# First modulation vectors of a Hyena-FFN block: five of eight row tiles on TensorE, three on VectorE

## The chip, the cores and the metric

The kernel runs on one core of one Trainium2 chip. The metric is the device time of one execution in microseconds; lower is better.

## The reference

The whole block is one adaLN-modulated Hyena mixer followed by a gated convolutional FFN, on x of 1024 positions by 1024 channels. What the change touches is the beginning:

```
mod = silu(c) @ mod_w + mod_b          # (1024,) @ (1024, 6*1024): six vectors of 1024
sh1, sc1, g1, sh2, sc2, g2 = split(mod, 6)
h_lat = rmsnorm(x, norm_g[0]) * (1 + sc1) + sh1
proj = short_conv(h_lat @ w_in + b_in, ...)

# filter network, on 33 position features, width 64
h = sin(freq * (pos @ f_w1 + f_b1))
h = sin(freq * (h @ f_w2 + f_b2))
h = sin(freq * (h @ f_w3 + f_b3))
h = h @ f_wout                          # then a decay, an FFT convolution, and so on
```

## The kernel before

All of it is one program. Each engine works through its own list of instructions in order, and a scheduler makes these lists from the order in which the code is written; where one engine needs another's result it waits for a semaphore.

The program begins with three things woven into each other. The first is the filter network (`filter_mlp`): three layers, each over two halves of 512 positions. A half of a layer is a matmul into a PSUM bank `mlp`, an activation on ScalarE that scales and biases it (`pre`), the reduction of the phase to one period, and the sine (`hs`). The reduction rounds `pre`/(2 pi) by adding a large number and subtracting it again (`n`, lines 259 and 260, both on VectorE), subtracts `n` times 2 pi in two steps (line 262) and clamps (line 263). After the third layer the result is split into a rounded and a rest part, `s_h` and `s_l`.

The second is the first two modulation vectors (`mods_start`): chunk 1 of `mod` (the scale, kept as the tile `mod1`) and then chunk 0 (the shift, `mod0`). The matrix of a chunk comes in as 16 tiles of 128 rows by 512 columns; `mw1_20` is chunk 1, row tile 2, column half 0. TensorE multiplies six of the eight row tiles by silu(c) into a PSUM row per column half (`ms`), VectorE the other two (`DV0`, `DV1`) into `msa` (lines 337 and 339). Then VectorE adds the PSUM row into partition 0 of `msa` (line 329, the fold), eight matmuls with a column of ones (`mv`, line 348) sum over the partitions and turn the row into columns, and `mod_fin` adds the bias (line 300); for chunk 1 it also multiplies by the norm's weight (line 302). A float32 matmul stands in the trace as two passes, so ten `ms` matmuls are a row of x20.

The third is the normalization of the first four tiles of x (`first_pre`, `first_norm`): ScalarE squares and sums (`junk`, line 369), VectorE and ScalarE form the root and scale x (`n10r`, lines 356 to 377), TensorE transposes (`n10p`, line 384), and ScalarE and VectorE apply both modulation vectors (`n10t`) and split the result into `hTh` and `hTl`. With these the main matmuls begin (`in8p`), and they go on to the end of the program.

SP issues the loads in the order of the table `ORDER`: chunk 1, four tiles of x, chunk 0 with one weight tile in between, and so on. The two lines that say which row tiles VectorE takes are

```
DV0 = (6, 7)
DV1 = (0, 1)
```

Of the kernel before, what the change touches and what calls it, by code (L numbers as in the profile page):

```python
# [10 lines left out]
F32 = mybir.dt.float32  # L11
F32R = mybir.dt.float32r
AF = mybir.ActivationFunctionType
ALU = mybir.AluOpType
# [4 lines left out]
D = 1024  # L19
# [3 lines left out]
KT = D // 128  # L23
EPS = 1e-6
MAGIC = 12582912.0
# [2 lines left out]
PI_LO = 3.1415925  # L28


ORDER = [("m", 1, 0, 8), ("x", 0, 4), ("m", 0, 0, 6), ("w", 1), ("m", 0, 6, 8), ("w", 2), ("x", 4, 8)]
DV0 = (6, 7)
DV1 = (0, 1)
XA = (1, 5, 7)
OFF = {
    "k": (0, 1, 2, 2, 3), "s": (0, 1, 2, 2, 3), "a": (0, 1, 2, 4), "b": (0, 1, 2, 3, 3, 4, 4, 5, 5, 6),
# [11 lines left out]
class Kern:  # L48
# [188 lines left out]
    def filter_mlp(self):  # L237
        nc, a, sp = self.nc, self.a, self.sp
        fv = self.fv
# [6 lines left out]
            nc.vector.tensor_copy(out=s[0:64, :, 64:128], in_=zv)  # L246
            nc.vector.tensor_copy(out=s[64:128, :, 0:64], in_=zv)

        fb = self.cp.tile([128, 3], F32, name="fb")
        nc.vector.tensor_scalar(out=fb, in0=fv[:, 0:3], scalar1=fv[:, 3:4], scalar2=None, op0=ALU.mult)  # L250
        cur = [self.pos[hf][0:66] for hf in range(2)]
        for ly, w in enumerate(self.fw):
            for hf in range(2):
                p = self.bank("ax", f"mlp{hf}{ly}")
                nc.tensor.matmul(out=p, lhsT=w, rhs=cur[hf], start=True, stop=True)
                pre = self.rp(f"pre{hf}{ly}")[:, 0:512]
                nc.scalar.activation(out=pre, in_=p, func=AF.Identity, scale=fv[:, 3:4], bias=fb[:, ly:ly + 1])
                n = self.ftile("o", f"n{hf}{ly}")
                nc.vector.tensor_scalar(out=n, in0=pre, scalar1=1.0 / (2 * math.pi), scalar2=MAGIC, op0=ALU.mult, op1=ALU.add)
                nc.vector.tensor_scalar(out=n, in0=n, scalar1=MAGIC, scalar2=None, op0=ALU.subtract)  # L260
                for c in (C1, C2):
                    nc.vector.scalar_tensor_tensor(out=pre, in0=n, scalar=-c, in1=pre, op0=ALU.mult, op1=ALU.add)
                nc.vector.tensor_scalar(out=pre, in0=pre, scalar1=PI_LO, scalar2=-PI_LO, op0=ALU.min, op1=ALU.max)
                h = self.ftile("t1", f"hs{hf}{ly}", bufs=2)
                nc.scalar.activation(out=h, in_=pre, func=AF.Sin)
                cur[hf] = h
# [10 lines left out]
    def mod_gen(self, ch, tags):  # L277
        nc, a = self.nc, self.a
        acc = self.rp(f"macc{ch}") if self.fp else self.op.tile([128, D], F32, tag="bc0", name=f"macc{ch}")
        for kt in range(KT):  # L280
# [6 lines left out]
            if kt == KT - 1:  # L287
                if ch in (3, 4):
                    p = self.bank("ax", f"mv{ch}")
                    for j in range(KT):  # L290
                        nc.tensor.matmul(out=p[:, j:j + 1], lhsT=acc[:, j * 128:j * 128 + 128], rhs=self.ones[:, 0:1], start=True, stop=True)
                    self.mod_fin(ch, p)
                else:
                    self.mod_row(ch, acc)
            yield 1

    def mod_fin(self, ch, p):
        nc = self.nc
        t = self.mshift[ch]
        nc.vector.tensor_tensor(out=t, in0=p[:, 0:KT], in1=self.modb[:, ch], op=ALU.add)  # L300
        if ch in (1, 4):
            nc.vector.scalar_tensor_tensor(out=t, in0=t, scalar=1.0, in1=self.ng[:, ch // 4], op0=ALU.add, op1=ALU.mult)

    def mod_row(self, ch, acc):
        nc = self.nc
# [15 lines left out]
    def mods_start(self, ch, dv):  # L321
# [2 lines left out]
        acc = [self.ftile("hl"[h], f"msa{ch}{h}") for h in range(2)]  # L324
        pe = [kt for kt in range(KT) if kt not in dv]

        def fold():
            for h in range(2):
                nc.vector.tensor_tensor(out=acc[h][0:1], in0=ps[h][0:1], in1=acc[h][0:1], op=ALU.add)

        for kt in range(KT):
            if kt == dv[-1] > pe[-1]:
                fold()
            for h in range(2):
                wv = self.msw[ch, kt, h]
                if kt == dv[0]:
                    nc.vector.tensor_scalar(out=acc[h], in0=wv, scalar1=self.scl[:, kt:kt + 1], scalar2=None, op0=ALU.mult)
                elif kt in dv:
                    nc.vector.scalar_tensor_tensor(out=acc[h], in0=wv, scalar=self.scl[:, kt:kt + 1], in1=acc[h], op0=ALU.mult, op1=ALU.add)
                else:  # L340
                    nc.tensor.matmul(out=ps[h][0:1], lhsT=self.scl[:, kt:kt + 1], rhs=wv, start=kt == pe[0], stop=kt == pe[-1])
        if pe[-1] > dv[-1]:
            fold()
        p = self.bank("ax", f"mv{ch}")
        for h in range(2):
            for j in range(4):
                js = slice(j * 128, j * 128 + 128)
                nc.tensor.matmul(out=p[:, h * 4 + j:h * 4 + j + 1], lhsT=acc[h][:, js], rhs=self.ones[:, 0:1], start=True, stop=True)
        self.mod_fin(ch, p)

    def rstd(self, ss, n, name):
        nc, cp = self.nc, self.cp
# [41 lines left out]
    def first_loads(self):  # L394
# [7 lines left out]
        for step in ORDER:  # L402
# [4 lines left out]
                    self.nc.sync.dma_start(out=self.xin[t], in_=a["x"][t * 128:t * 128 + 128])  # L407
            else:
                _, ch, k0, k1 = step
                for kt in range(k0, k1):  # L410
                    for h in range(2):
                        w = self.htile(n // 4, n % 4 // 2, "hl"[n % 2], f"mw{ch}_{kt}{h}", F32)
                        n += 1
                        c0 = ch * D + h * 512
                        nc.sync.dma_start(out=w, in_=a["mod_w"][kt * 128:kt * 128 + 128, c0:c0 + 512])
                        self.msw[ch, kt, h] = w
        self.wo = self.sp.tile([128, D], F32, tag="delta", name="wo")
        nc.sync.dma_start(out=self.wo[0:64], in_=a["hy_f_wout"][:, 0:D])
        nc.sync.dma_start(out=self.wo[64:128], in_=a["hy_f_wout"][:, D:2 * D])
# [1096 lines left out]
```

## Time and profile before

| | |
|---|---|
| median of 3 runs | 1305.76 us (1305.61 to 1305.9) |
| profiled execution, its own time | 1301.95 us |
| its span, first to last instruction | 1300.2 us |
| TensorE matmul busy | 1232.0 us, 95% of the span |
| VectorE busy | 1063.9 us, 82% |
| ScalarE busy | 744.0 us, 57% |

The profiled execution is one run of the program; its span leaves out 1.75 us of its time that lie around the first and last instruction. A timeline lists one engine's instructions by start time, with those of one kind merged; in brackets stand the engine's idle time before them and what ended it. The table of stretches gives, for each stretch of time, how long each engine was busy, the clock that TensorE was granted (1.00 is the upper of its two levels, 0.50 the lower) and the mean busy share of the DMA engines.

### The profile page before, as it was taken

The page shows a single profiled execution, that of the slowest core. Times are in us where ns is not written, and L with a number is a line of the kernel's source. Part 1 is how long each engine was busy: PE and PEld are TensorE (multiplying, and loading weights), DVE is VectorE, ACT ScalarE, POOL GpSimd, SP SyncE. Part 2 cuts the span into 40 slices and gives each one's busy share as a digit, 9 for nine tenths or more (in the row PEclk, how much of TensorE's full clock was granted, in tenths as well). Part 3 has the DMA queues.
Part 4 walks back from the last instruction along what each step waited for, and adds up shares of the span by engine and source line. Part 5 has one row for each costly group of instructions (what it writes and reads, how often), then busy time and mean ns, then how long its engine had stood idle before and what let it go on. Part 6 is the DMA issues. An engine that isn't in the chain of part 4 may idle for free. (4 is left out here: it accounts for less than half of the span.)

```text
span 1300.2 us, 16048 instructions
## 1 busy us (share of the span) xinstructions
PE 1232.0 (95%) x5368; PEld 971.7 (75%) x5368; DVE 1063.9 (82%) x1351; ACT 744.0 (57%) x1215; POOL 353.2 (27%) x292
## 2 busy tenths in 40 slices
PE   7999989999899999999989999999999999998976
PEld 2687767777677777878768878888888878886865
DVE  7899875578786998796989998788778798977996
ACT  4798866677676878553644444444544454425442
POOL 2000011012100210000086445455445301521461
PEclk9999999999999999999989999999999999999988
DMA  9555699989989997543124431222222388646542
GB/s 339 191 156 156 209 287 285 275 251 269 270 253 301 273 302 263 175 154 128 51 83 129 161 129 65 98 81 76 87 81 82 130 286 307 232 154 219 197 144 97
DMA packets 112400, 241.35 MB, mean 186 GB/s; under 512 B 12436, under 2 KB 25620, under 8 KB 112318
## 3 DMA queue, kind: packets, MB, share of 16 engines
q1 hardware_dynamic: 96790, 226.83, 53.4%
q0 software_dynamic: 14848, 13.39, 4.9%
q8 instruction: 42, 0.69, 0.2%
q14 instruction: 40, 0.33, 0.1%
q10 hardware_dynamic: 680, 0.12, 0.0%
HBM read 186.29 MB, written 54.00 MB: 185 GB/s over the span
## 5 line engine op out<-in xcount | busy, mean ns | idle before, releaser
L1010 DVE SCALAR_TENSOR_TENSOR facc<-fpad,v_ffn_conv_w,facc 128x1024 f32<-128x1024 f32 x176 | 225.2, 1285 | 22.8 <-ACT facc L1005 19.2
L62 ACT ACTIVATE dh<-dr 128x512 fp32r<-128x512 f32 x132 | 75.7, 623 | 64.0 <-PE dB L58 23.4
L63 DVE TENSOR_TENSOR dl<-dr,dh 128x512 fp32r<-128x512 f32 x132 | 102.8, 825 | 4.2 <-ACT dh L62 4.0
L507 POOL DMA_DIRECT2D k_b<-in_k_b_dram x64 | 34.0, 532 | 263.6 <-PE ks L59 177.3
L973 POOL TENSOR_TENSOR s<-wrua 128x512 f32<-128x512 f32 x21 | 29.3, 1396 | 188.2 <-DVE s12l L963 95.6
L57 PE MATMUL dA<-dh,dh 128*128 128x512 f32 x176 | 69.7, 396 | 8.7 <-DVE p5fpad L1311 7.7
L58 PE MATMUL dA<-dl,dh 128*128 128x512 f32 x176 | 69.2, 393 | 2.0 <-DVE dl L63 2.0
L963 POOL TENSOR_TENSOR s43l<-s,s43h 128x1024 fp32r<-128x1024 f32 x21 | 50.4, 2399 | 68.5 <-ACT s43h L962 68.5
L59 PE MATMUL dA<-dh,dl 128*128 128x512 f32 x176 | 68.9, 392 | 0.0
L58 PE MATMUL dB<-dl,dh 128*128 128x512 f32 x132 | 52.2, 395 | 5.1 <-DVE dl L63 5.1
L59 PE MATMUL dB<-dh,dl 128*128 128x512 f32 x132 | 51.9, 393 | 0.0
L57 PE MATMUL dB<-dh,dh 128*128 128x512 f32 x132 | 51.9, 393 | 0.0
L58 PE MATMUL op<-wlo,qh 128*128 128x512 f32 x128 | 50.3, 393 | 0.0
L57 PE MATMUL op<-who,qh 128*128 128x512 f32 x128 | 50.0, 393 | 0.0
L59 PE MATMUL op<-who,ql 128*128 128x512 f32 x128 | 49.9, 390 | 0.0
L1005 ACT ACTIVATE facc<-fpad,v_ffn_conv_b,v_ffn_conv_w 128x1024 f32<-128x1024 f32 x22 | 26.6, 1210 | 37.4 <-DVE fpad L1073 37.3
L57 PEld LDWEIGHTS dA<-dh,dh 128*128 128x128 f32 x176 | 33.5, 191 | 16.4 <-issue 8.1
L286 DVE SCALAR_TENSOR_TENSOR macc<-mw,scl,macc 128x1024 f32<-128x1024 f32 x28 | 38.1, 1361 | 9.4 <-DMA mw<-in_mod_w_dram 9.2
L507 POOL DMA_DIRECT2D k_bi<-in_k_bi_dram x32 | 17.1, 534 | 103.3 <-PE zd L59 47.6
L962 ACT ACTIVATE s12h<-s 128x1024 fp32r<-128x1024 f32 x21 | 22.3, 1061 | 39.6 <-PE s L58 35.3
L974 POOL TENSOR_TENSOR s<-s,wrug 128x512 f32<-128x512 f32 x21 | 42.8, 2039 | 1.5
L573 ACT ACTIVATE who<-wro,invn 128x512 fp32r<-128x512 f32 x32 | 21.8, 717 | 37.1 <-PE op L59 28.7
(585 smaller groups left out, 4050.4 us busy)
## 6 DMA issues: line engine op xcount, KB each, us to landing
dr<-du SPq DMA_DIRECT2D x66, 256.0 KB, 3.7
dr<-in_ffn_w_down_dram SPq DMA_DIRECT2D x66, 256.0 KB, 4.6
mw<-in_mod_w_dram SPq DMA_DIRECT2D x32, 512.0 KB, 4.6
wrin<-in_hy_w_in_dram SPq DMA_DIRECT2D x24, 512.0 KB, 6.4
wrug<-in_ffn_w_up_dram SPq DMA_DIRECT2D x22, 512.0 KB, 3.4
wrua<-in_ffn_w_up_dram SPq DMA_DIRECT2D x22, 512.0 KB, 4.7
du<-fs SPq DMA_DIRECT2D x22, 512.0 KB, 2.6
mw<-in_mod_w_dram SPq DMA_DIRECT2D x32, 256.0 KB, 6.5
```

The costliest lines, as they stand in the source:

```text
L57: mm(out=out, lhsT=lh, rhs=rh, start=start, stop=False, **kw)
L58: mm(out=out, lhsT=lh, rhs=rl, start=False, stop=False, **kw)
L59: mm(out=out, lhsT=ll, rhs=rh, start=False, stop=stop, **kw)
L62: self.nc.scalar.activation(out=hi, in_=src, func=AF.Copy)
L63: self.nc.vector.tensor_tensor(out=lo, in0=src, in1=hi.bitcast(F32), op=ALU.subtract)
L286: nc.vector.scalar_tensor_tensor(out=acc, in0=w, scalar=self.scl[:, kt:kt + 1], in1=acc, op0=ALU.mult, op1=ALU.add)
L507: self.nc.gpsimd.dma_start(out=b, in_=self.a[name][k2])
L963: eng.tensor_tensor(out=l, in0=src, in1=h.bitcast(F32), op=ALU.subtract)
L973: tt(out=s12[:, lo], in0=a[:, lo], in1=a[:, hi], op=ALU.add)
L974: tt(out=s12[:, hi], in0=s12[:, lo], in1=g[:, lo], op=ALU.subtract)
L1005: nc.scalar.activation(out=av, in_=pad[:, 1:17, 1:65], func=AF.Identity, scale=self.cw[:, b, 4:5], bias=self.cb[:, b:b + 1])
L1010: nc.vector.scalar_tensor_tensor(out=av, in0=pad[:, dy:dy + 16, dx:dx + 64], scalar=self.cw[:, b, i:i + 1], in1=av, op0=ALU.mult, op1=ALU.add)
```

## The change

Row tiles move from TensorE to VectorE: of each chunk VectorE takes three and TensorE five. In the filter network the subtraction of the large number goes from VectorE to ScalarE, as an activation with a bias tile (`fb[:, 3:4]`, filled by a memset). `mod_fin` works on a slice of columns, and `mods_start` folds, multiplies by ones and finishes the first column half ahead of the second. For chunk 0 the tiles that VectorE takes are loaded by column halves: 50, 60, 70, and then 51, 61, 71, behind the weight tile.

```
-ORDER = [("m", 1, 0, 8), ("x", 0, 4), ("m", 0, 0, 6), ("w", 1), ("m", 0, 6, 8), ("w", 2), ("x", 4, 8)]
-DV0 = (6, 7)
-DV1 = (0, 1)
+ORDER = [("m", 1, 0, 8), ("x", 0, 4), ("m", 0, 0, 5), ("w", 1), ("m", 0, 5, 8), ("w", 2), ("x", 4, 8)]
+DV0 = (5, 6, 7)
+DV1 = (0, 1, 2)
...
-        fb = self.cp.tile([128, 3], F32, name="fb")
-        nc.vector.tensor_scalar(out=fb, in0=fv[:, 0:3], scalar1=fv[:, 3:4], scalar2=None, op0=ALU.mult)
+        fb = self.cp.tile([128, 4], F32, name="fb")
+        nc.vector.memset(fb[:, 3:4], -MAGIC)
+        nc.vector.tensor_scalar(out=fb[:, 0:3], in0=fv[:, 0:3], scalar1=fv[:, 3:4], scalar2=None, op0=ALU.mult)
...
-                nc.vector.tensor_scalar(out=n, in0=n, scalar1=MAGIC, scalar2=None, op0=ALU.subtract)
+                nc.scalar.activation(out=n, in_=n, func=AF.Identity, bias=fb[:, 3:4])
...
-                    self.mod_fin(ch, p)
+                    self.mod_fin(ch, p, slice(0, KT))
...
-    def mod_fin(self, ch, p):
+    def mod_fin(self, ch, p, c):
         nc = self.nc
-        t = self.mshift[ch]
-        nc.vector.tensor_tensor(out=t, in0=p[:, 0:KT], in1=self.modb[:, ch], op=ALU.add)
+        t = self.mshift[ch][:, c]
+        nc.vector.tensor_tensor(out=t, in0=p[:, c], in1=self.modb[:, ch, c], op=ALU.add)
...
-        def fold():
+        def fold(h):
+            nc.vector.tensor_tensor(out=acc[h][0:1], in0=ps[h][0:1], in1=acc[h][0:1], op=ALU.add)
+
+        for kt in range(KT):
             for h in range(2):
-                nc.vector.tensor_tensor(out=acc[h][0:1], in0=ps[h][0:1], in1=acc[h][0:1], op=ALU.add)
-
-        for kt in range(KT):
-            if kt == dv[-1] > pe[-1]:
-                fold()
-            for h in range(2):
+                if kt == dv[-1] > pe[-1]:
+                    fold(h)
...
-        if pe[-1] > dv[-1]:
-            fold()
         p = self.bank("ax", f"mv{ch}")
         for h in range(2):
+            if pe[-1] > dv[-1]:
+                fold(h)
             for j in range(4):
                 js = slice(j * 128, j * 128 + 128)
                 nc.tensor.matmul(out=p[:, h * 4 + j:h * 4 + j + 1], lhsT=acc[h][:, js], rhs=self.ones[:, 0:1], start=True, stop=True)
-        self.mod_fin(ch, p)
+            self.mod_fin(ch, p, slice(h * 4, h * 4 + 4))
...
-                for kt in range(k0, k1):
-                    for h in range(2):
+                for kt, h in sorted(((kt, h) for kt in range(k0, k1) for h in range(2)), key=lambda x: x[1] if k0 else x[0]):
```

From line 250 up to `mod_fin` the changed kernel's line numbers are one higher (line 259 is 260 there, 263 is 264, 300 is 301); in `mods_start` they are the same. The scheduler makes new lists from the changed code. The first 870 rows of TensorE's list differ in places, the rest stands in the same order. Three places matter below.

The first is TensorE in layers 1 and 2 of the filter network (`mlp01` is half 0 of the second layer, `mlp11` half 1). Before:

```order
L341 MATMUL ms10_309<-mw1_20_148,scl_79 1x512
L341 MATMUL ms11_310<-mw1_21_150,scl_79 1x512
L341 MATMUL ms10_309<-mw1_30_152,scl_79 1x512
L341 MATMUL ms11_310<-mw1_31_154,scl_79 1x512
L341 MATMUL ms10_309<-mw1_40_156,scl_79 1x512
L255 MATMUL mlp01_253<-hs00_239,fw_102 128x512
L341 MATMUL ms11_310<-mw1_41_158,scl_79 1x512
L255 MATMUL mlp11_265<-hs10_251,fw_102 128x512
```

In the change:

```order
L341 MATMUL ms10_310<-mw1_30_152,scl_79 1x512
L341 MATMUL ms11_311<-mw1_31_154,scl_79 1x512
L341 MATMUL ms10_310<-mw1_40_156,scl_79 1x512
L341 MATMUL ms11_311<-mw1_41_158,scl_79 1x512
L256 MATMUL mlp01_254<-hs00_240,fw_102 128x512
L256 MATMUL mlp11_266<-hs10_252,fw_102 128x512
```

The tiles `mw1_20` and `mw1_21` have left TensorE's list, and both matmuls of the second layer now stand together behind four `ms` matmuls; before they stood behind five and six, one apart.

The second place is VectorE around the third layer (`pre02`, `n02`: half 0; `pre12`, `n12`: half 1). Before:

```order
L329 TENSOR_TENSOR msa10_311<-ms10_309,msa10_311 1x512
L259 TENSOR_SCALAR n02_281<-pre02_279 128x512
L260 TENSOR_SCALAR n02_281<-n02_281 128x512
L262 SCALAR_TENSOR_TENSOR pre02_279<-n02_281,pre02_279 128x512
L259 TENSOR_SCALAR n12_293<-pre12_291 128x512
L262 SCALAR_TENSOR_TENSOR pre02_279<-n02_281,pre02_279 128x512
L260 TENSOR_SCALAR n12_293<-n12_293 128x512
L263 TENSOR_SCALAR pre02_279<-pre02_279 128x512
L262 SCALAR_TENSOR_TENSOR pre12_291<-n12_293,pre12_291 128x512
L329 TENSOR_TENSOR msa11_312<-ms11_310,msa11_312 1x512
```

In the change:

```order
L329 TENSOR_TENSOR msa10_312<-ms10_310,msa10_312 1x512
L329 TENSOR_TENSOR msa11_313<-ms11_311,msa11_313 1x512
L301 TENSOR_TENSOR mod1_82<-mv1_330,v_mod_b_118 128x4
L303 SCALAR_TENSOR_TENSOR mod1_82<-mod1_82,v_norm_g_120 128x4
L260 TENSOR_SCALAR n02_282<-pre02_280 128x512
L301 TENSOR_TENSOR mod1_82<-mv1_330,v_mod_b_118 128x4
L303 SCALAR_TENSOR_TENSOR mod1_82<-mod1_82,v_norm_g_120 128x4
L260 TENSOR_SCALAR n12_294<-pre12_292 128x512
L263 SCALAR_TENSOR_TENSOR pre02_280<-n02_282,pre02_280 128x512
L263 SCALAR_TENSOR_TENSOR pre12_292<-n12_294,pre12_292 128x512
L263 SCALAR_TENSOR_TENSOR pre02_280<-n02_282,pre02_280 128x512
L263 SCALAR_TENSOR_TENSOR pre12_292<-n12_294,pre12_292 128x512
```

Both folds and the finishing of chunk 1 (lines 301 and 303) now stand ahead of the rounding steps of the third layer; before, the second fold and the finishing stood behind them. ScalarE's list at the same place, before:

```order
L369 ACTIVATE junk_347,n10ss_342<-xin2_134 128x1024
L369 ACTIVATE junk_349,n10ss_342<-xin3_135 128x1024
L265 ACTIVATE hs02_287<-pre02_279 128x512
L274 ACTIVATE s_h_219<-hs02_287 64x8x16x4 x2
L265 ACTIVATE hs12_299<-pre12_291 128x512
L274 ACTIVATE s_h_219<-hs12_299 64x8x16x4 x2
```

In the change:

```order
L261 ACTIVATE n02_282<-n02_282,fb_227 128x512
L261 ACTIVATE n12_294<-n12_294,fb_227 128x512
L369 ACTIVATE junk_350,n10ss_345<-xin2_134 128x1024
L369 ACTIVATE junk_352,n10ss_345<-xin3_135 128x1024
L266 ACTIVATE hs02_288<-pre02_280 128x512
L266 ACTIVATE hs12_300<-pre12_292 128x512
L275 ACTIVATE s_h_219<-hs02_288 64x8x16x4 x2
L275 ACTIVATE s_h_219<-hs12_300 64x8x16x4 x2
```

The two new activations stand first, then two squares of x tiles, then both sines, then the four copies into `s_h`; before, half 0 had its sine and its copies ahead of half 1's sine.

The third place is VectorE at chunk 0, from the first row tile to the last weight split. Before:

```order
L337 TENSOR_SCALAR msa00_367<-mw0_60_202,scl_79 128x512
L63 TENSOR_TENSOR wlin8_398<-wrin8_200,whin8_397 128x1024
L337 TENSOR_SCALAR msa01_368<-mw0_61_204,scl_79 128x512
L329 TENSOR_TENSOR msa00_367<-ms00_365,msa00_367 1x512
L329 TENSOR_TENSOR msa01_368<-ms01_366,msa01_368 1x512
L339 SCALAR_TENSOR_TENSOR msa00_367<-mw0_70_206,scl_79,msa00_367 128x512
L339 SCALAR_TENSOR_TENSOR msa01_368<-mw0_71_208,scl_79,msa01_368 128x512
L63 TENSOR_TENSOR wlin16_490<-wrin16_210,whin16_489 128x1024
```

In the change:

```order
L337 TENSOR_SCALAR msa00_370<-mw0_50_198,scl_79 128x512
L63 TENSOR_TENSOR wlin8_402<-wrin8_196,whin8_401 128x1024
L339 SCALAR_TENSOR_TENSOR msa00_370<-mw0_60_200,scl_79,msa00_370 128x512
L337 TENSOR_SCALAR msa01_371<-mw0_51_204,scl_79 128x512
L329 TENSOR_TENSOR msa00_370<-ms00_368,msa00_370 1x512
L339 SCALAR_TENSOR_TENSOR msa01_371<-mw0_61_206,scl_79,msa01_371 128x512
L339 SCALAR_TENSOR_TENSOR msa00_370<-mw0_70_202,scl_79,msa00_370 128x512
L329 TENSOR_TENSOR msa01_371<-ms01_369,msa01_371 1x512
L339 SCALAR_TENSOR_TENSOR msa01_371<-mw0_71_208,scl_79,msa01_371 128x512
L63 TENSOR_TENSOR wlin16_494<-wrin16_210,whin16_493 128x1024
L301 TENSOR_TENSOR mod0_81<-mv0_390,v_mod_b_118 128x4
```

Ahead of the first `mv` matmul, which needs `msa00` complete, there stood one multiply-add and two folds behind the first products; now there stand three multiply-adds and one fold.

## Rows read from the trace of the kernel before

**Rows 1.** The page: its head and the TensorE row of part 1.

```profile
span 1300.2 us, 16048 instructions
...
PE 1232.0 (95%) x5368; PEld 971.7 (75%) x5368; DVE 1063.9 (82%) x1351; ACT 744.0 (57%) x1215; POOL 353.2 (27%) x292
```

**Rows 2.** Timeline of TensorE, 0 to 50 us: start, length, instructions, wait before.

```profile
10.20 6.49 PE L341 MATMUL ms<-mw,scl 128*1 128x512 f32 x10 [0.97 <-DMA mw<-in_mod_w_dram]
...
18.62 1.13 PE L255 MATMUL mlp<-hs,fw 128*128 128x512 f32 x2
...
25.21 1.13 PE L255 MATMUL mlp<-hs,fw 128*128 128x512 f32 x2
...
31.44 8.74 PE L341 MATMUL ms<-mw,scl 128*1 128x512 f32 x20
42.39 0.38 PE L348 MATMUL mv<-ones,msa 128*128 128x1 f32 x2 [2.20 <-DVE msa L339]
...
43.97 1.62 PE L348 MATMUL mv<-ones,msa 128*128 128x1 f32 x14
45.85 0.66 PE L384 MATMUL n10p<-v_eye,xin 128*128 128x128 f32 x4 [0.26 <-DVE mod L300]
...
48.38 0.48 PE L57 MATMUL in8p<-hTh,whin 128*128 128x512 f32 x1
```

**Rows 3.** Timeline of TensorE's weight loads, 9 to 45 us.

```profile
12.72 0.13 PEld L341 LDWEIGHTS ms<-mw,scl 128*1 128x1 f32 x1 [0.73 <-DMA mw<-in_mod_w_dram]
13.57 0.13 PEld L341 LDWEIGHTS ms<-mw,scl 128*1 128x1 f32 x1 [0.73 <-issue]
14.38 0.09 PEld L341 LDWEIGHTS ms<-mw,scl 128*1 128x1 f32 x1 [0.68 <-DMA mw<-in_mod_w_dram]
14.81 0.08 PEld L341 LDWEIGHTS ms<-mw,scl 128*1 128x1 f32 x1 [0.34 <-issue]
```

**Rows 4.** Timeline of VectorE, 0 to 90 us.

```profile
25.32 0.68 DVE L329 TENSOR_TENSOR msa<-ms,msa 1x512 f32<-1x512 f32 x1 [1.41 <-PE ms L341]
...
26.36 0.43 DVE L260 TENSOR_SCALAR n<-n 128x512 f32<-128x512 f32 x1
...
27.43 0.51 DVE L259 TENSOR_SCALAR n<-pre 128x512 f32<-128x512 f32 x1
...
36.48 2.08 DVE L377 TENSOR_SCALAR xin<-xin,n10r 128x1024 f32<-128x1024 f32 x3
38.47 0.48 DVE L337 TENSOR_SCALAR msa<-mw,scl 128x512 f32<-128x512 f32 x1
38.87 1.22 DVE L63 TENSOR_TENSOR wlin<-wrin,whin 128x1024 fp32r<-128x1024 f32 x1
...
40.40 1.27 DVE L329 TENSOR_TENSOR msa<-ms,msa 1x512 f32<-1x512 f32 x2
41.60 1.39 DVE L339 SCALAR_TENSOR_TENSOR msa<-mw,scl,msa 128x512 f32<-128x512 f32 x2
```

**Rows 5.** Timeline of ScalarE, 0 to 90 us.

```profile
28.22 1.06 ACT L369 ACTIVATE junk<-xin 128x1024 f32<-128x1024 f32 x1
...
31.98 0.63 ACT L265 ACTIVATE hs<-pre 128x512 f32<-128x512 f32 x1 [0.78 <-DVE pre L263]
32.64 1.28 ACT L274 ACTIVATE s_h<-hs 64x512 fp32r<-64x512 f32 x2
33.94 1.28 ACT L356 ACT_TABLE_LOAD   x1
...
64.32 0.69 ACT L606 ACTIVATE pad<-in8p,v_hy_b_in 128x512 f32<-128x512 f32 x1
```

**Rows 6.** Timeline of TensorE, 654 to 668 us.

```profile
660.97 0.80 PE L57 MATMUL uz<-b22hl,s43h 128*128 128x512 f32 x1 [6.40 <-ACT pu L1065]
661.56 0.63 PE L58 MATMUL uz<-b22hl,s43h 128*128 128x512 f32 x1
...
666.30 0.39 PE L57 MATMUL s<-tT3h,s43h 128*128 128x512 f32 x1
```

**Rows 7.** Busy time by stretch: span, engines, TensorE's granted clock, DMA share, GB/s.

```profile
661.00:664.00 3.00, 3.00 (x7) 2.21 (x8) 3.00 (x3) 1.98 (x3) 1.59 (x2) 0.50 0.20 81
```

**Rows 8.** Busy time by stretches of 20 us, columns as in rows 7.

```profile
60.00:80.00 20.00, 20.00 (x99) 16.43 (x99) 16.56 (x22) 19.02 (x30) 0.00 (x0) 1.00 0.52 159
...
140.00:160.00 20.00, 20.00 (x84) 15.26 (x83) 17.75 (x26) 18.33 (x33) 0.00 (x0) 1.00 0.70 223
...
320.00:340.00 20.00, 15.98 (x67) 12.40 (x68) 12.97 (x19) 11.54 (x20) 3.57 (x7) 1.00 0.99 268
```

More of the change, by code (lines that the diff above doesn't have):

```diff
@@ L295, in mod_gen @@
             yield 1
-    def mod_fin(self, ch, p):
+    def mod_fin(self, ch, p, c):
         nc = self.nc
-        t = self.mshift[ch]
-        nc.vector.tensor_tensor(out=t, in0=p[:, 0:KT], in1=self.modb[:, ch], op=ALU.add)
+        t = self.mshift[ch][:, c]
+        nc.vector.tensor_tensor(out=t, in0=p[:, c], in1=self.modb[:, ch, c], op=ALU.add)
         if ch in (1, 4):
-            nc.vector.scalar_tensor_tensor(out=t, in0=t, scalar=1.0, in1=self.ng[:, ch // 4], op0=ALU.add, op1=ALU.mult)
+            nc.vector.scalar_tensor_tensor(out=t, in0=t, scalar=1.0, in1=self.ng[:, ch // 4, c], op0=ALU.add, op1=ALU.mult)
     def mod_row(self, ch, acc):
@@ L409, in first_loads @@
                 _, ch, k0, k1 = step
-                for kt in range(k0, k1):
-                    for h in range(2):
[L412 to L416, printed above, removed]
+                for kt, h in sorted(((kt, h) for kt in range(k0, k1) for h in range(2)), key=lambda x: x[1] if k0 else x[0]):
+                    w = self.htile(n // 4, n % 4 // 2, "hl"[n % 2], f"mw{ch}_{kt}{h}", F32)
+                    n += 1
+                    c0 = ch * D + h * 512
+                    nc.sync.dma_start(out=w, in_=a["mod_w"][kt * 128:kt * 128 + 128, c0:c0 + 512])
+                    self.msw[ch, kt, h] = w
         self.wo = self.sp.tile([128, D], F32, tag="delta", name="wo")
```

## The prediction

> **What bounds the kernel now.** I read the page first. TensorE is busy for 1232.0 of 1300.2 us [rows 1]. Then the table of stretches: from 60 to 160 us TensorE is busy for the whole of every stretch [rows 8], so whatever shifts the first main matmul shifts everything behind it, until the stretches in which TensorE waits again for transfers (15.98 busy of 20 us at 320 us, with a DMA share of 0.99). The change is all ahead of that first main matmul, at 48.38 us [rows 2], so I read the timelines of the three engines up to there and ask what is late at each step.
>
> The reader is to see two different heads. Up to the last layer-3 matmul at 25.21 us TensorE has almost no gap. From there VectorE and ScalarE decide: the last sine is at 31.98, the table load at 33.94 [rows 5], the scaling of x at 36.48 [rows 4]. TensorE has finished chunk 0's row tiles at 31.44 + 8.74 = 40.18 and then stands empty for 2.20 us until VectorE's `msa` is complete [rows 2]. So at the end of the head TensorE waits for VectorE, not the other way round.
>
> **The change part by part.** I place the new lists' instructions one behind the other with the durations of the rows. An instruction on VectorE follows an independent one after its length less about 0.08 us and a dependent one 0.04 us after its end.
>
> *Layers 1 and 2.* VectorE gets two more multiply-adds of 0.7 us (1.39 for two) and loses two roundings of 0.43 [rows 4]; ScalarE gets the new activation. That has no row before; the nearest is the biased copy at 64.32, 0.69 us, and a plain one of 0.63 is the lower bound [rows 5]. I take 0.69. This makes the layer-1 sines about 0.7 us later, and that is covered, because TensorE comes to its second-layer matmuls later still. It now begins with `mw1_30`, whose weight load ran at 12.72 [rows 3], and does four `ms` matmuls, eight passes. A pass took 0.85 us up to 14.38 (12.72, 13.57) and 0.43 from there on [rows 3]; these are the two levels of its clock. All eight at the upper level end at 16.1, all eight at the lower at 19.5. TensorE did 4.2 us of unbroken work from 10.20 on before its pace rose [rows 2, 3]; here it stands empty until 12.7, so I take about half of them slow: 17.9. The second layer's matmuls follow, 1.06 apart: the last starts at 19.0, before at 18.62 [rows 2]. From there to the last layer-3 matmul it was 25.21 - 18.62 = 6.59 us. Now both halves go in step (the lists alternate them), their sines come together, and the two matmuls stand back to back: 7.2 us, so 26.2. **Together +1.0 us** (-0.3 if the clock is up at once, +2.7 if it comes up only after the four matmuls).
>
> *Layer 3.* Between that matmul and the scaling of x lay 36.48 - 25.21 = 11.27 us. Now VectorE finishes chunk 1 ahead of the rounding. The first four `mv` matmuls come behind the last layer-3 matmul and end at 28.2 (fourteen passes took 1.62, so a pass is 0.11 [rows 2], and a matmul two). Two small operations follow (lines 301, 303). The second four `mv` matmuls write the same PSUM bank, and in the built program the first of them waits for line 301 of the first half: the halves do not overlap, they alternate. Half 1's rounding, at 27.43 before [rows 4], so comes at 29.75. It is 0.43, then 0.69 on ScalarE, then three multiply-adds' steps and two clamps to 33.5. ScalarE does two squares of 1.06 plus reading the sum [rows 5] in between, which end at 33.3 and cost nothing more. Half 1's sine starts at 33.75 (before 31.98). Then four copies of 0.65 (32.64 for two: 1.28), of which two lay ahead of it before: the table load is at 37.0 instead of 33.94 [rows 5], and x is scaled 36.48 - 33.94 = 2.54 later, at 39.5. **+2.0 us here, +3.0 in all.**
>
> *Chunk 0.* From the scaling to the first `mv` it was 42.39 - 36.48 = 5.91. VectorE has the same three scalings (2.08), two first products (0.40 a step) and one weight split (1.14) [rows 4], and three multiply-adds (0.66) and one fold (0.60) in place of one and two: 2 x 0.66 - 0.60 = **+0.7**, so 46.1. The four `ms` matmuls fewer give TensorE 4 x 0.87 = 3.5 us [rows 2], and it only waits longer for VectorE: they cover nothing. From the first `mv` to `in8p` it was 48.38 - 42.39 = 5.99. Finishing the first half early lets `n10t` begin earlier and takes TensorE's wait of 0.26 before the fourth transposition [rows 2] away, against a new wait of about 0.3 for line 301 between the halves: **-0.4**, `in8p` at 51.7.
>
> *The clock.* The ten `ms` matmuls of chunk 0 start behind the second `mv`, at 29.4, and end at 38.0. TensorE is then empty until 46.1: 8 us. The trace has such a place: after 6.40 us without work the matmuls at 660.97 to 666.30 come 0.43 us apart, the granted clock is 0.50, and the upper level is back at 666.30 [rows 6, 7]. Those 12 matmuls took 5.33 us instead of 12 x 0.23, 2.6 us more. The 2.20 us before did not do this [rows 2]. So the transpositions and first main matmuls run at the lower level. Lower bound 0 (the work there waits for VectorE and ScalarE anyway), upper 2.6. I take **+1.5**, because some of the slow passes lie under the waits for lines 301 and `n10t`. The Trainium skill has this as a rule (TensorE: Matmul & The Clock Gate, "What's actually happening"): the lower clock is the default, sustained activity lifts it, and idleness brings it back. By the rows the sum has this term; by a reading that the clock stays up, which the 2.20 us would allow, it would be +3.3 instead of +4.8.
>
> *Loads.* SP issues as many bytes; the weight tile moves two tiles ahead and VectorE's tiles behind it. VectorE's first product followed the scaling without a wait at 38.47 [rows 4], so the tiles were there, and they are wanted later now: nothing.
>
> *The rest.* +4.8 at `in8p` passes through the full stretches to 160 us. Behind them some of it falls into waits for transfers that end when they end: between 0 and all of it; I take 0.5, since those loads are mostly asked for by the delayed work itself. The memset (128x1) and the smaller finishing operations are nothing.
>
> **Sum:** +1.0 +2.0 +0.7 -0.4 +1.5 -0.5 = **+4.3 us**, in the profiled execution 1301.95 + 4.3 = 1306.25. The median of the runs is 1305.76, 3.8 us above the profiled execution, so the forecast is **1310.1 us**. A measurement tells about 0.2% (2.6 us) from no change.
>
> **Rivals.**
> *The clock stays up.* TensorE reaches the upper level as early as before and does not fall in the gap. For it: the 2.20 us gap left no trace. Against it: the 6.40 us gap did. The terms are then -0.3 +2.0 +0.7 -0.4 to +1.0 +2.0 +0.7 -0.4, so +2.0 to +3.3: 1307.8 to 1309.1.
> *Absorbed.* The later start is given back between 160 and 500 us, where TensorE waits for transfers. For it: the DMA share of 0.99 and 4 us of idle time in one stretch. Against it: the transfers there are asked for by matmul results that are late too. 1305.8 to 1306.5. The scheduler's other order up to row 870 could do the like, in either direction.
> *TensorE was the bound: faster.* If TensorE's queue set the pace of the head, the four `ms` matmuls that have left it (two per chunk, chunk 1's ahead of chunk 0's) would move `in8p` up by 4 x 0.87 = 3.5 us: 1302.3. For it: the fold at 25.32 waited 1.41 us for TensorE [rows 4], and its row tiles run without a gap from 31.44. Against it: the gap of 2.20 us right behind them. It decides if the first `mv` of chunk 0 stands before 42.39.
>
> **How the numbers follow.** The forecast's case (path longer, clock falls) 0.62, its own range 1308.4 to 1313.0. Clock stays up 0.15, half of it below 1308.4. Absorbed 0.15, mostly within 0.2%. TensorE the bound, or a better order further on, 0.08. Slower by over 0.2%: 0.58 + 0.08 + 0.03 = 0.69; within: 0.04 + 0.07 + 0.10 + 0.03 = 0.24; faster: 0.02 + 0.05 = 0.07. The range 1305.9 to 1313.0 leaves out the faster cases and what exceeds the sum's upper bounds.
>
> **What the profile would show.** The weight load of `mw1_30` first on TensorE, near 12.7, and 0.85 us passes behind it beyond 14.38. Half 1's rounding in layer 3 behind line 303. The table load near 37 instead of 33.94, the scaling of x near 39.5, the first `mv` of chunk 0 near 46, with a TensorE gap of some 8 us before it, transpositions 0.22 us apart instead of 0.11 behind it, and `in8p` near 53. From 60 to 160 us TensorE full. I am wrong in the first terms if the scaling of x is before 38, in the clock if the passes behind the gap are 0.11 apart, and in the last if `in8p` is late and the end is not.

## The result and the profile after

The changed kernel is slower: median 1314.8 us (1310.99 to 1320.35, 9 runs) against 1305.61 us, a ratio of 1.0071 with a 95% interval of 1.0049 to 1.0093, or 9.3 us. Run once more among the experiments it gave 1.0052 (1.0031 to 1.0072), or 6.8 us; the medians there, 1313.97 and 1304.76 us, lie 9.2 us apart. The forecast was 4.3 us more, with 7.2 as its upper end. The direction was right; the forecast had about half of the size that was measured first.

The profiled execution after took 1319.68 us, one of the longest. The page's head and its TensorE row answer to [rows 1]:

```profile
span 1317.9 us, 16035 instructions
...
PE 1239.4 (94%) x5360; PEld 981.7 (74%) x5360; DVE 1062.4 (81%) x1353; ACT 747.6 (57%) x1221; POOL 354.9 (27%) x292
```

TensorE's timeline after, as [rows 2]:

```profile
12.77 5.37 PE L341 MATMUL ms<-mw,scl 128*1 128x512 f32 x8 [2.55 <-DMA mw<-in_mod_w_dram]
18.07 1.99 PE L256 MATMUL mlp<-hs,fw 128*128 128x512 f32 x4
...
28.25 1.05 PE L348 MATMUL mv<-ones,msa 128*128 128x1 f32 x8 [0.26 <-DVE mod L301]
29.23 10.44 PE L341 MATMUL ms<-mw,scl 128*1 128x512 f32 x20
45.90 0.59 PE L348 MATMUL mv<-ones,msa 128*128 128x1 f32 x2 [6.23 <-DVE msa L339]
46.35 2.80 PE L384 MATMUL n10p<-v_eye,xin 128*128 128x128 f32 x12
48.94 1.28 PE L348 MATMUL mv<-ones,msa 128*128 128x1 f32 x6
50.48 1.86 PE L348 MATMUL mv<-ones,msa 128*128 128x1 f32 x8 [0.26 <-DVE mod L301]
52.20 4.51 PE L384 MATMUL n10p<-v_eye,xin 128*128 128x128 f32 x20
56.36 0.78 PE L57 MATMUL in8p<-hTh,whin 128*128 128x512 f32 x1
```

The reader is to see two losses. The first `mv` of chunk 0 stands at 45.90 instead of 42.39, behind an empty TensorE of 6.23 us instead of 2.20. From there to `in8p` it takes 10.46 us instead of 5.99; nothing new stands between them, but each pass takes twice as long (20 transpositions in 4.51 us). The table of stretches, columns as in [rows 7], shows the granted clock there:

```profile
40.00:44.00 4.00, 0.00 (x0) 0.00 (x0) 4.00 (x8) 3.35 (x5) 0.00 (x0) 0.96 1.05 332
44.00:48.00 4.00, 2.10 (x10) 2.10 (x11) 3.96 (x6) 0.00 (x0) 0.00 (x0) 0.50 0.64 173
48.00:52.00 4.00, 3.75 (x20) 3.66 (x19) 1.34 (x3) 1.54 (x3) 0.00 (x0) 0.50 0.38 131
52.00:56.00 4.00, 4.00 (x20) 4.00 (x21) 2.83 (x6) 3.25 (x6) 0.00 (x0) 0.50 0.01 2
56.00:60.00 4.00, 4.00 (x18) 3.36 (x17) 3.33 (x9) 3.86 (x8) 0.00 (x0) 0.83 0.00 0
...
140.00:160.00 20.00, 20.00 (x85) 15.50 (x84) 19.31 (x28) 17.51 (x32) 0.00 (x0) 1.00 0.59 185
```

TensorE is at 0.50, its lower level of 1.2 GHz, from inside the empty stretch until some main matmuls have run, although it is busy for 3.75 and 4.00 of 4 us. Behind that TensorE is busy all the time again (19.69 of 20 us from 60 to 80, then 20.00 up to 160), as in [rows 8], so the delay stays.

VectorE's and ScalarE's timelines, as [rows 4] and [rows 5]; these are the places named in the prediction:

```profile
28.23 0.16 DVE L303 SCALAR_TENSOR_TENSOR mod<-mod,v_norm_g 128x4 f32<-128x4 f32 x1
...
29.53 0.16 DVE L303 SCALAR_TENSOR_TENSOR mod<-mod,v_norm_g 128x4 f32<-128x4 f32 x1
29.61 0.42 DVE L260 TENSOR_SCALAR n<-pre 128x512 f32<-128x512 f32 x1
...
39.27 2.08 DVE L377 TENSOR_SCALAR xin<-xin,n10r 128x1024 f32<-128x1024 f32 x3
```

```profile
30.07 0.72 ACT L261 ACTIVATE n<-n,fb 128x512 f32<-128x512 f32 x1 [0.50 <-DVE n L260]
...
36.73 1.28 ACT L356 ACT_TABLE_LOAD   x1
```

### The profile page after: what moved, and what is told of

The parts are those of the page before. It is cut to its first block, busy times and chain, and to the rows that moved or that the text cites. A ratio compares the mean times of both kernels' runs of the same rounds, so it can differ in the third digit from the quotient of the medians.

```text
span 1317.9 us, 16035 instructions
## 1 busy us (share of the span) xinstructions
PE 1239.4 (94%) x5360; PEld 981.7 (74%) x5360; DVE 1062.4 (81%) x1353; ACT 747.6 (57%) x1221; POOL 354.9 (27%) x292
## 4 chain that ended last, share of the span: by engine, by line
PE 64%; DMA 12%; DVE 10%; issue 7%; ACT 5%; POOL 1%; SPq 0%; ACTq 0%; DVEq 0%; POOLq 0%
PE s L57 5%; PE s L58 5%; PE s L59 5%; DMA mw<-in_mod_w_dram 3%; PE uz L57 3%; PE uz L59 3%; PE uz L58 3%; PE dA L57 2%; PE dA L58 2%; PE dA L59 2%; DMA k_bi<-in_k_bi_dram 2%; PE dB L58 2%; PE dB L57 2%; PE dB L59 2%; DVE dl L63 2%
```

## The experiments

Theory 1 says that the change costs at two places ahead of `in8p`: the path of VectorE and ScalarE to the first `mv` of chunk 0, and behind it the lower clock, into which the waiting TensorE falls. The rivals name one part of the change, the halves' wait for each other, or the lists and transfers further on. One table holds what is read from each run: the first `mv` of chunk 0, TensorE's empty time just before it, the first `in8p` and the first `in9p` (all us), and the ratio to the kernel before on the same chip. Behind `in9p` TensorE is full up to 160 us.

| run | first mv | empty | in8p | in9p | ratio (95%) |
|---|---|---|---|---|---|
| before | 42.39 | 2.20 | 48.38 | 75.61 | |
| after | 45.90 | 6.23 | 56.36 | 84.11 | 1.0071 (1.0049 to 1.0093) |
| e7_again | 46.22 | 7.93 | 56.68 | 84.81 | 1.0052 (1.0031 to 1.0072) |
| e1_vec_round | 44.75 | 4.37 | 54.93 | 86.67 | 1.0089 (1.0061 to 1.0118) |
| e2_two_rows | 43.87 | 4.68 | 53.70 | 81.53 | 1.0054 (1.0032 to 1.0075) |
| e3_whole | 46.94 | 9.15 | 57.41 | 84.50 | 1.0085 (1.0054 to 1.0116) |
| e4_fill | 47.10 | 1.06 | 53.16 | 84.93 | 1.0079 (1.0051 to 1.0107) |
| e5_prio | 46.40 | 6.23 | 55.15 | 84.86 | 1.0077 (1.0048 to 1.0107) |
| e6_prio_fill | 46.99 | none | 52.93 | 82.09 | 1.0055 (1.0032 to 1.0078) |
| e8_fill_six | 47.31 | 2.78 | 52.50 | 81.28 | 1.0047 (1.0024 to 1.0069) |
| e9_prio_again | 45.98 | 6.23 | 54.73 | 84.32 | 1.0060 (1.0038 to 1.0082) |
| b1_round | 45.03 | 5.90 | 52.75 | 79.98 | 1.0030 (1.0011 to 1.0050) |
| b2_rows | 46.97 | 7.58 | 56.80 | 88.58 | 1.0093 (1.0059 to 1.0126) |
| b3_halves | 41.78 | 1.25 | 47.42 | 75.09 | 0.9982 (0.9961 to 1.0004) |
| b4_one_row | 41.73 | 1.43 | 48.83 | 76.24 | 0.9983 (0.9965 to 1.0002) |
| b5_weight_late | 42.39 | 0.97 | 48.39 | 78.13 | 1.0004 (0.9986 to 1.0023) |
| b6_halves_one_row | 40.62 | 0.97 | 46.27 | 73.96 | 1.0002 (0.9977 to 1.0027) |

The beginning varies from trace to trace: in e8 and e9, whose lists on TensorE agree up to there, chunk 1's first `mv` stands at 28.45 and at 27.12. So a difference of 1 us or so between two rows says little by itself. In e5, e6, e8 and e9 the first `in8p` stands behind 24 of the 32 transpositions, in the others behind all.

### Filling the wait

**e4_fill**, the changed kernel with

```
+        if ch == 0:
+            w = self.bank("mm", "warm")
+            for i in range(8):
+                nc.tensor.matmul(out=w[0:1], lhsT=self.scl[:, 0:1], rhs=self.msw[0, 0, 0], start=True, stop=True)
         p = self.bank("ax", f"mv{ch}")
```

> The changed kernel, with eight extra matmuls on TensorE between chunk 0's last row-tile matmul and its first matmul with ones; they multiply a row tile once more into a spare PSUM bank that nobody reads, 8 x 0.87 = 7.0 us of work in a wait of 8 us, so the output is untouched. Theory 1 (the empty TensorE loses its upper clock, and the transpositions behind the wait run at the lower one): the passes behind the first matmul with ones are 0.11 us apart, the first in8p is near 52 instead of 56.36, and the kernel takes about 4.5 us less than the changed one, near 1310, still slower than before by some 4 to 5 us. Rival A (the transpositions only follow VectorE and ScalarE, which are late): in8p stays near 56 and the time near 1314.8 whatever the clock does. Rival B (the loss lies in the other order and the transfers further on): in8p may move, the end does not.

TensorE's timeline, and under it ScalarE's:

```profile
39.01 7.03 PE L345 MATMUL warm<-mw,scl 128*1 128x512 f32 x16
47.10 0.38 PE L352 MATMUL mv<-ones,msa 128*128 128x1 f32 x2 [1.06 <-DVE msa L339]
47.34 1.51 PE L388 MATMUL n10p<-v_eye,xin 128*128 128x128 f32 x12
...
51.00 2.40 PE L388 MATMUL n10p<-v_eye,xin 128*128 128x128 f32 x20 [0.26 <-DVE mod L301]
53.16 0.48 PE L57 MATMUL in8p<-hTh,whin 128*128 128x512 f32 x1
...
65.46 1.70 PE L388 MATMUL n11p<-v_eye,xin 128*128 128x128 f32 x12 [0.69 <-ACT xin L379]
69.20 3.17 PE L388 MATMUL n11p<-v_eye,xin 128*128 128x128 f32 x16 [2.04 <-ACT n11t L391]
```

```profile
66.46 1.28 ACT L463 ACT_TABLE_LOAD   x1
67.76 0.72 ACT L463 ACTIVATE dec<-delta,tneg 128x512 f32<-128x512 f32 x1
68.39 1.43 ACT L391 ACTIVATE n11t<-n11p,mod,mod 128x512 f32<-128x512 f32 x2
```

The clock stayed at its upper level and `mv` to `in8p` took 6.06 us instead of 10.46: the transpositions do not wait for VectorE and ScalarE, which refutes rival A. The time did not follow: theory 1's number for it missed. The extra matmuls had moved the scheduler's lists, ScalarE now did a table load and a `dec` ahead of the `n11t` that TensorE wanted, and by `in9p` the lead was gone. The waits of 0.69 and 2.04 us were not all of it: behind them the granted clock was 0.50 once more (70 to 72 us), and the last 16 `n11p` took 3.17 us instead of the 1.96 of the changed kernel. So two partners were run whose lists agree with each other but for single rows.

**e5_prio** and **e6_prio_fill**, both with the first edit, the second also with the eight matmuls:

```
+            with tc.high_priority():
+                self.first_pre(1)
+                self.first_norm(1)
```

> The changed kernel, with the normalization of the second four tiles of x put ahead in the lists by the scheduler's priority. It is the partner of the next run: in the run with the extra matmuls ScalarE's list had come out otherwise behind in8p (a table load and a dec ahead of n11t), and TensorE waited 0.69 and 2.04 us for it; with the priority the lists of both partners are the same row for row but for one row of VectorE. Theory 1: TensorE is empty for 6 us before chunk 0's first matmul with ones as in the changed kernel, the transpositions are 0.22 apart and the first in8p is at 56 to 57; the time is that of the changed kernel within 3 us.

> As the run before, with the eight extra matmuls between chunk 0's last row-tile matmul and its first matmul with ones, whose result nobody reads. Theory 1 (the lower clock behind the empty TensorE delays all that follows): passes 0.11 apart, the first in8p 3 to 4 us earlier than in the partner, the same lead still there at 80 and 160 us, and a time 3 to 4 us less than the partner's. Rival F (the lead is lost again because VectorE and ScalarE, which make the operands of the first main matmuls, did not come earlier by as much): in8p is earlier but the lead is under 1 us by 80 us, and the times agree within 1.5 us.

The lead is 2.2 us at `in8p` and 2.8 at `in9p` (84.86 against 82.09), and TensorE's first `ks` (167.53 and 164.74) still shows it; the ratios differ by 0.0022, with intervals that overlap. Eight matmuls also ended so late that they put the first `mv` off. **e8_fill_six** has six, **e9_prio_again** is the partner once more:

> The changed kernel with the priority for the second four tiles of x, and six extra matmuls (5.2 us) in TensorE's wait where the run with eight had put off the first matmul with ones by 0.6 us. Theory 1: the extra matmuls end before VectorE's msa is there, so the first matmul with ones is where the partner without them has it (46.4), behind a wait near 1 us; passes 0.11 apart; in8p 2.5 to 4 us ahead of the partner's and the lead still there at 160 us; the time 2 to 4 us below that of the partner in this job. Rival F: the lead is in the trace at in8p and no longer in the time.

> The partner once more, with the priority and no extra matmuls, beside the run with six on the same chip: by theory 1 2 to 4 us over it, with the clock down from some 44 to some 58 us; by rival F within 1.5 us of it.

TensorE's timelines, with six extra matmuls and then without:

```profile
39.22 5.31 PE L346 MATMUL warm<-mw,scl 128*1 128x512 f32 x12
47.31 0.38 PE L353 MATMUL mv<-ones,msa 128*128 128x1 f32 x2 [2.78 <-DVE msa L340]
47.55 1.51 PE L389 MATMUL n10p<-v_eye,xin 128*128 128x128 f32 x12
...
52.50 0.48 PE L57 MATMUL in8p<-hTh,whin 128*128 128x512 f32 x1
```

```profile
45.98 0.59 PE L349 MATMUL mv<-ones,msa 128*128 128x1 f32 x2 [6.23 <-DVE msa L340]
46.43 2.80 PE L385 MATMUL n10p<-v_eye,xin 128*128 128x128 f32 x12
...
54.73 0.78 PE L57 MATMUL in8p<-hTh,whin 128*128 128x512 f32 x1
```

From the first `mv` to `in8p` it is 5.19 against 8.75 us, 3.6 less with the upper clock, on nearly the same lists. (The run with six is later from its first `ms` matmuls on, whose eight passes took 6.48 us against 5.40; chunk 1's first `mv`, at 28.45 there and at 27.12 in the partner, is 18.86 us ahead of chunk 0's in both.) At `in9p` the lead is 3.0. The ratios differ by 0.0013, 1.7 us: both pairs have the sign of theory 1, but neither resolves a difference this small, so what the clock alone costs in device time is not shown by them.

### One part undone

**e1_vec_round** restores `nc.vector.tensor_scalar(out=n, in0=n, scalar1=MAGIC, scalar2=None, op0=ALU.subtract)`; **e2_two_rows** restores `DV0 = (6, 7)`, `DV1 = (0, 1)` and the old `ORDER`; **e3_whole** restores the fold, `mod_fin` and the loads of whole vectors.

> The changed kernel with one part undone: the large number is subtracted on VectorE again (0.43 us) and not on ScalarE (0.69 us); three row tiles and the column halves stay. Theory 1: the third layer comes out by 1 to 2 us earlier, since the two halves no longer run in step, but VectorE's third row tile keeps the first matmul with ones of chunk 0 at 44 to 45.5, TensorE is still empty for over 5 us before it, the clock falls, and the kernel gains 0.5 to 2 us on the changed one. Rival C (the step on ScalarE with its reordering is the whole cost): the first matmul with ones returns to 42.4 or 43, the wait shrinks to 3 us, the clock stays, and the time comes within 0.2% of before.

> The changed kernel with one part undone: VectorE takes two row tiles of each chunk again and TensorE six; the rounding on ScalarE and the column halves stay. Theory 1: VectorE's list is 0.7 us shorter per chunk and TensorE's 3.5 us longer in all, so the first matmul with ones of chunk 0 is near 44 to 45, but the wait before it only 3 to 4 us; whether the clock falls in a wait of that length no row has shown (2.20 us kept it, 6.23 lost it). If it stays, in8p is near 50 and the time 3 us above before; if it falls, near 54. Rival D (the third row tile on VectorE is the whole cost): the time is that of before.

> The changed kernel with one part undone: both column halves are folded, multiplied with ones, finished and loaded together, as before; three row tiles and the rounding on ScalarE stay. Theory 1: the wait for line 301 between the halves goes (0.26 us, twice) and the finishing of chunk 1 is two operations fewer, but VectorE's path to the first matmul with ones and the wait of TensorE stay, the clock falls, and the time is that of the changed kernel within 1.5 us. Rival E (the halves, by waiting for each other, are what delays the finish of chunk 0 and with it in8p): in8p is 3 us or more earlier than 56.36 and the time follows.

With the rounding back on VectorE the first `mv` is 1.2 us earlier, as expected, behind a wait of 4.37 us (over 5 was expected), and TensorE still falls to the lower clock, against rival C. The gain was not there at the end, though: here, too, ScalarE's list has the table load ahead of `n11t`, TensorE waits 0.70 and 2.04 us for it, and `in9p` is 2.6 us later than in the changed kernel. So this run does not take away the rounding alone. With two rows the wait of 4.68 us also ended in the lower clock, with `in8p` near the 54 named for that, and a ratio of 1.0054: the third row is not the whole cost (against rival D). With whole vectors nothing gets better, against rival E.

### One part alone, on the kernel before

> The kernel before with one part of the change alone: the large number is subtracted on ScalarE; two row tiles on VectorE and whole vectors as before. In the built program both halves of the second and third layers now run in step and chunk 1 is finished ahead of the third layer's rounding. Theory 1 (this reordering by itself delays the third layer by some 2 us, and TensorE, which has nothing else, falls to the lower clock): the first matmul with ones of chunk 0 near 44.5 instead of 42.39, a wait of 4 to 5 us before it, in8p at 53 to 54, time 5 to 7 us over before. Rival G (an activation of 0.69 for an operation of 0.43 costs 0.3 us a layer and nothing more): in8p within 1 us of 48.38 and the time within 0.2% of before.

> The kernel before with one part of the change alone: VectorE takes three row tiles of each chunk and TensorE five; the rounding stays on VectorE and the vectors stay whole. Theory 1: VectorE's path to the first matmul with ones of chunk 0 grows by about 1.4 to 2.5 us and TensorE's wait before it from 2.20 to about 7 us, the clock falls, in8p at 54 to 56, time 6 to 9 us over before. Rival H (only the two extra multiply-adds count, 0.7 us a chunk): in8p at 49.5 to 50, time within 0.2% of before. Rival I (the time of the change is a sum of its parts, and each has its share): this run and the one with the rounding alone add up to the 9.2 us of the whole change; by theory 1 they add up to more, since each alone already drops the clock.

> The kernel before with one part of the change alone: the column halves are folded, multiplied with ones, finished and loaded one ahead of the other; two row tiles on VectorE, the rounding on VectorE. Theory 1 (the clock falls where VectorE's path to chunk 0's first matmul with ones grows by two us or more): nothing is added on that path, TensorE's wait before it stays near 2 us, the clock stays up, in8p within 1 us of 48.38, and the time is that of before within 0.2%. Rival E (the halves wait for each other over the shared PSUM bank): in8p 1 to 3 us later.

The rounding on ScalarE alone costs 3.9 us: the first `mv` is 2.6 later, behind an empty stretch of 5.90 us. The interval, 1.4 to 6.5 us, reaches into the 5 to 7 expected; `in8p` came at 52.75 instead of 53 to 54, since the clock came back earlier, here in the table of stretches:

```profile
44.00:48.00 4.00, 2.97 (x14) 2.97 (x15) 2.77 (x4) 0.39 (x2) 0.00 (x0) 0.50 0.74 185
48.00:52.00 4.00, 3.59 (x29) 3.27 (x28) 1.70 (x3) 1.80 (x3) 0.00 (x0) 0.92 0.30 115
```

The third row alone costs 12.1 us (7.7 to 16.5), above the 6 to 9 expected. The lower clock is there, and ScalarE's order of e4 once more, in TensorE's timeline:

```profile
46.97 0.59 PE L348 MATMUL mv<-ones,msa 128*128 128x1 f32 x2 [7.58 <-DVE msa L339]
...
69.10 1.70 PE L384 MATMUL n11p<-v_eye,xin 128*128 128x128 f32 x12 [0.70 <-ACT xin L375]
72.84 3.36 PE L384 MATMUL n11p<-v_eye,xin 128*128 128x128 f32 x16 [2.04 <-ACT n11t L387]
```

The first `mv`, too, is later than expected, by 4.6 us instead of 1.4 to 2.5: as in e1, ScalarE here does a second table load of 1.28 us ahead of the last sine, and VectorE three `s_l` splits (2.12 us) between the scaling of x and `msa`, which neither the kernel before nor the changed one does there. So b2 is not the third row alone. Rounding and rows add up to 16.0 us against 9.3 and 6.8 of the whole, and at `in8p` to 12.8 against 8.0, so the time is not a sum of such parts (against rival I): each already drops the clock, and b2 has an order that costs by itself. The halves alone cost nothing, and `in8p` is 1.0 us earlier with them in that trace.

### The other direction

**b4_one_row** is the kernel before with `DV1 = (0,)`, **b5_weight_late** with `("m", 0, 0, 8), ("w", 1), ("w", 2)` in `ORDER`, **b6_halves_one_row** joins b3 and b4.

> The kernel before with a step in the opposite direction: of chunk 1 VectorE takes one row tile and TensorE seven; chunk 0 as before. Theory 1 (VectorE's list sets the first matmul with ones of chunk 0, TensorE's does not, as long as it is not empty for long): VectorE loses two multiply-adds, 1.4 us, ahead of the third layer, TensorE gains 1.74 us that lie in its work before 25.2 us; the first matmul with ones within 1 us of 42.39, the clock stays, and the time is that of before within 0.2%. By the rival that TensorE's list sets the head (the one that had the changed kernel faster) it is 1.7 us or more later.

> The kernel before with the first weight tile loaded behind all tiles of chunk 0: in the built lists its split, 1.14 us on VectorE, then stands behind chunk 0's finish and not inside it. Theory 1 (VectorE's list sets the head): the first matmul with ones at 41.2 to 41.5 instead of 42.39, TensorE's wait near 1 us, in8p at 47.3 if the split, now ahead of the hTl's, does not delay it, at 48.4 if it does; the time 0 to 1 us less than before, too little to tell by the clock on the wall, so the trace decides. Against: the lists differ further on too, as in the changed kernel.

> The kernel before with the column halves (taken alone 0.9982, interval 0.9961 to 1.0004) and one row tile of chunk 1 on VectorE instead of two (taken alone 0.9983, 0.9965 to 1.0002). If the two gains are real and add up, the ratio to before is near 0.9965 and its interval ends below 1; in the trace the first matmul with ones of chunk 0 stands 0.6 to 1.3 us ahead of 42.39. If each was chance, or both shorten the same stretch, the ratio is between 0.998 and 1.000.

With TensorE's list of chunk 1 longer by one row the first `mv` is 0.7 us earlier, where the rival had it 1.7 or more later, and TensorE still waits 1.43 us for VectorE ahead of it: TensorE did not set the head. b6 has it 1.8 us ahead and `in8p` 2.1:

```profile
40.62 0.38 PE L347 MATMUL mv<-ones,msa 128*128 128x1 f32 x2 [0.97 <-DVE msa L338]
...
46.27 0.48 PE L57 MATMUL in8p<-hTh,whin 128*128 128x512 f32 x1
```

But its ratio is 1.0002; the 0.998 of b3 and b4 did not add up. No version was found that beats the kernel before by more than the measurement tells. In b5 the wait shrank to 0.97 us, but the first `mv` stands at 42.39 again, not at the 41.2 to 41.5 expected, and `in8p` came no earlier. That trace was already 1.2 us late ahead of it: x is scaled at 37.71 instead of 36.48, and from there to the first `mv` it takes 4.68 us instead of 5.91, much as expected.

### The changed kernel again

> The changed kernel itself once more, unchanged, for a second trace of it. The first one lasted 1319.68 us, among the longest of its runs, and what it lost behind in8p (from 8.0 us at in8p to 17.7 at the end) may be that run's own. Theory 1: up to in8p this trace agrees with the first within 0.5 us, with the clock down from some 44 to some 57; behind 400 us it differs by several us, and the median over before is 8 to 10 us. Rival B (the order and the transfers further on cost what is missing): the steps of 2 to 4 us between 400 and 450 us and at the end stand at the same places again.

TensorE's timeline:

```profile
29.55 8.74 PE L341 MATMUL ms<-mw,scl 128*1 128x512 f32 x20
46.22 0.58 PE L348 MATMUL mv<-ones,msa 128*128 128x1 f32 x2 [7.93 <-DVE msa L339]
...
52.52 4.51 PE L384 MATMUL n10p<-v_eye,xin 128*128 128x128 f32 x20
```

Up to `in8p` the second trace is the first one within 0.33 us, with the same 10.46 us from the first `mv` on. The wait ahead of it is 7.93 us here, the 8 that were forecast, and was 6.23 in the first trace, because there the same 20 `ms` passes took 10.44 us instead of 8.74: the granted clock was 0.50 from 31 to 33 us, shortly behind the 16 one-column passes of chunk 1; here it was 1.00 at that place. That cost nothing, since TensorE waited for VectorE anyway. The span of the second trace is 1312.0 instead of 1317.9 us, so some 6 us of what the first one lost further on were that execution's own. The trace of before is itself a short one: b3, b4 and b5 have ratios of 0.998 to 1.000 and spans of 1303.4 to 1304.5 against its 1300.2. The step between `in1p` and `in4p`, which rival B asked for, does stand again (2.5 us more than in before at first, now 3.1), but b3 and b4, which lost no time, also fall 4.0 and 5.6 us behind that one trace between `in15p` and `op`. So what these single traces show behind `in9p` cannot be pinned on the change, and whether that step costs anything stays open.

## Why the prediction was right in its direction and wrong in its size

The sum by its own terms, read from the traces:

| term | forecast | measured | from |
|---|---|---|---|
| layers 1 to 3 | +3.0 | +2.8 | scaling of x at 39.27, before 36.48 |
| chunk 0 to the first mv | +0.7 | +0.7 | 45.90 - 39.27 = 6.63, before 5.91 |
| mv to in8p, upper clock | -0.4 | +0.1 | 53.16 - 47.10 = 6.06 (e4), before 5.99 |
| clock | +1.5 | +4.4 | 10.46 - 6.06 |
| in8p | +4.8 | +8.0 | 56.36, before 48.38 |

**The path was right.** Each place up to the first `mv` came within 0.3 us: the four `ms` matmuls end at 18.1 (forecast 17.9), half 1's rounding at 29.61 behind line 303 (29.75), the table load at 36.73 (37.0), the scaling at 39.27 (39.5), the first `mv` at 45.90 (46.1). That VectorE and ScalarE set the head, and not TensorE, is shown by b4.

**The clock was the step that failed**: "Lower bound 0 (the work there waits for VectorE and ScalarE anyway), upper 2.6. I take +1.5". The upper bound came from [rows 6], where twelve matmuls of 512 columns stand behind the wait and the upper level is back after 5.33 us. Behind chunk 0 stand matmuls of one column and transpositions. In the changed kernel, in both its traces, all of them ran at the lower level, 4.4 us longer than with the clock up in e4, and it rose only behind the first main matmuls. The other half of the sentence fell too: the waits for line 301 hide nothing, since line 301 itself waits for the slow `mv`. The Trainium skill (TensorE: Matmul & The Clock Gate, "Part 4: PE-mode transpose") says that the upper clock does not engage for transpositions. The change's traces agree (0.50 over 32 transpositions, with TensorE busy for 3.75 and 4.00 of 4 us), three other runs do not. In b1, where the same 12 transpositions come first and then 14 passes of one column, the upper level was back before the last 20 transpositions; in e1 and b2 it came back among these last 20; in e3, with the order of b1, it did not come back before `in8p`. TensorE's timelines of e1 and e3:

```profile
51.44 3.73 PE L383 MATMUL n10p<-v_eye,xin 128*128 128x128 f32 x20 [0.26 <-DVE mod L300]
```

```profile
53.23 4.53 PE L385 MATMUL n10p<-v_eye,xin 128*128 128x128 f32 x20 [0.26 <-DVE mod L301]
```

So from the first `mv` over 32 transpositions to `in8p` it took 5.64 to 6.06 us with the clock up and 7.72 (b1) to 10.47 us (e3) with it down. What decides when it comes back stays open.

**The -0.4** for finishing the first half early did not come in the changed kernel: b3 gains 0.3 us between the first `mv` and `in8p` (5.64 against 5.99), while e4, with the clock up, gains nothing.

**The -0.5 for absorption** is not seen: what TensorE is late at `in9p` is lost. Over the 16 runs of the table (after and the fifteen experiments), the time over before (ratio less 1, times 1305 us) against the delay of `in9p` over 75.61 gives a straight line of slope 1.08 with a correlation of 0.95 and a scatter of 1.5 us, less than the interval of any single ratio. That is too coarse to price 0.5 us, but leaves no room for a loss given back as a whole. By this line a delay made by the clock is in the time like any other; it is a correlation over different kernels, and the pairs with and without the extra matmuls agree with it without proving it. For the change it is 8.5 us (9.2 in the second trace), between the 9.3 and 6.8 us measured.

Of the rivals, the clock that stays up is refuted by the rows above, absorption by this line, TensorE as the bound by b4.

## What to carry to other kernels

A wait of TensorE can cost more than its length where small matmuls and transpositions stand behind it: take as the upper bound that all of them run at the lower clock up to the first large matmuls (4.4 us here; 1.7 in the mildest run), not the time at which large ones got it back elsewhere. Work moved off a waiting engine onto the one it waits for can cost twice, by its own length and by the lower clock behind the longer wait. And where a scheduler makes the lists, an experiment that adds work needs a partner with the same lists: here a lead of 3 us was gone 30 us later through one table load in another place.

## What the runs showed of the hardware

The clock also fell where TensorE was hardly empty. In b4, whose TensorE timeline follows, the wait before the first `mv` was 1.43 us, and yet the last 16 transpositions took 3.16 us instead of 1.97:

```profile
41.73 0.38 PE L348 MATMUL mv<-ones,msa 128*128 128x1 f32 x2 [1.43 <-DVE msa L339]
...
46.02 3.16 PE L384 MATMUL n10p<-v_eye,xin 128*128 128x128 f32 x16 [0.16 <-ACT n10t L387]
```

In e6, with no wait ahead of the first `mv` and two of 0.25 us behind it, the granted clock was 0.65 over 52 to 56 us. TensorE had done matmuls of one column and transpositions before both, and matmuls of one column before the fall near 31 us in the first trace of the change, which its second trace does not have. In e4 the clock fell behind a wait of 2.04 us, with transpositions on either side of it. Over a wait of 2.78 us in e8 the clock stayed up. So in this kernel the length of the wait alone did not decide it.
